# A transformer block on one core: the feed-forward operands are made once without the norm's factor, and its first column block takes the seven-product form too

## The chip, the cores and the metric

The kernel runs on one core of a Trainium2 chip. The core has a matrix engine (PE, which loads weights with its own instructions, PEld), a vector engine (DVE), an activation engine (ACT), a general engine (POOL), and queues that start transfers (SP's, POOL's, ACT's). In the trace each engine runs its instructions in the order in which the program lists them, and waits at an instruction until what it needs is there. The metric is the device time of one execution in microseconds. The kernel before takes 1032.63 us (median of 3 runs, 1032.61 to 1032.65).

## The reference, cut to what matters

256 tokens of width 2048 in fp32 pass one encoder layer:

```
xn = rms_norm(x) * g1;  proj = xn @ w_in        # q, k, v and the convolution's columns
h  = x + concat(attention, convolution) @ w_out
hn = h * rsqrt(mean(h*h) + eps) * g2            # the second norm
y  = h + (silu(hn @ w_gate) * (hn @ w_up)) @ w_down
```

`w_gate` and `w_up` are 2048 x 5632, `w_down` is 5632 x 2048. The factor `rsqrt(...)` is one number for each token. Call it r. It commutes with the product: `hn @ w_gate = r * ((h * g2) @ w_gate)`.

## The kernel before, in words

**Numbers.** Every fp32 operand is split in a high and a low part, and a product is three matmuls: high by high, low by high, high by low. Tokens stand in two halves of 128 (m = 0, 1). A matmul is always 128 x 128 by 128 x 512. The weights come from DRAM as fp32: ACT rounds a raw tile to its high part (`whi`, line 326), DVE subtracts for the low part (`wlo`, line 335); for some tiles the low part is made by ACT and an accumulating transfer of POOL's queue instead (lines 329, 330).

**Chunks.** The program is a list of chunks in the order of PE. A plain chunk is two row tiles of 128 of one weight by 512 columns: 12 matmuls. A loop in `run_chunks` emits, for chunk t, the loads, roundings and splits of the next two or three chunks and then the multiplication of t. Everything that follows from a finished sum (adds, transposes, norms) is a generator, and one step of each running generator is emitted at fixed places within each multiplication (`resume`). So the order on every engine is fixed by this emission, and nothing reorders it later.

**Feed-forward blocks.** There are 11 blocks of 512 hidden columns (j = 0 to 10), in groups of 4, 4 and 3, each group followed by its part of the `w_down` product. Blocks 1 to 10 use a seven-product form on half of the 16 row tiles: four "pairs" (kind s). A pair takes rows p and p + 8 of both `w_gate` and `w_up` and both token halves as a 2 x 2 by 2 x 2 product of tiles, with 7 products in place of 8, so 21 matmuls in place of 24. The other eight row tiles are plain chunks, four of gate (kind g) and four of up (kind u). `ORDER` and `FIRST_ORDER` are strings of these kinds, 12 chunks to a block. For a pair DVE makes sums of weight tiles (`wt`, lines 1049 to 1051), ACT rounds seven tiles (`wh`, lines 1052 and 1055), DVE makes the low parts `wlb` (line 1058) and `wlt` (line 1059). PE's third matmul of a pair reads `wlt`. The sums of the products lie in eight PSUM banks (Q1 to Q7, QX), four of the pool `acc` and four of `aux`. After a block's last pair, `bank_sums` combines banks (one ACT copy, six DVE adds); after its last chunk `block_done` adds two more, multiplies gate and up on DVE, and PE transposes the result (`ps_a`).

**Block 0 before.** It is plain: eight chunks of gate, then eight of up, 192 matmuls. Its token operands `hhi`, `hlo` are the transposed `h * g2`, without r. The silu takes r as its scale (line 876), the product with up takes it again (line 883).

**The operands of blocks 1 to 10 before.** While block 0 runs, `make_forms` builds them from `hn` (the transposed `h * g2`): it spreads r over the partitions by PE (`rep`, `ps_r`, `rb`), multiplies `hn` with it on DVE (line 996), rounds the plain ones (`chi`, `clo`) and builds the seven sums for the pairs (`sums`, `fhi`, `flo`).

**What lies ahead of it.** The product with `w_out` runs in four column blocks n = 0 to 3. For each finished one, `out_done(n)` adds the residual on DVE (line 828), transposes h on PE (`ps_h`, line 846), scales with g2 on ACT (line 851), splits, squares and sums h on ACT (line 479), and writes h to DRAM by POOL's queue (line 823). r exists only after n = 3.

## Time and profile before

| what | number |
|---|---|
| median of 3 runs | 1032.63 us |
| span of the profiled execution | 1030.8 us |
| PE busy, share of the span | 1025.7 us, 100% |
| DVE busy | 929.2 us, 90% |
| ACT busy | 643.4 us, 62% |
| POOL busy | 102.7 us, 10% |
| DMA, mean | 232 GB/s |

The span is 1.8 us short of the runs' median; the same offset is assumed on both sides of the change. Times in the prediction are microseconds from the start of the span. A row of the timeline gives start, duration, engine, line, operation, output<-input, size and count, and in brackets the idle time of the engine ahead of it with what ended it. Two instructions on one engine overlap at their ends, so what a queue takes is read from start to start, not from the durations.

### The profile page before, as it was taken

The numbers are of one execution on the slowest core, as the hardware profiler recorded it, in microseconds if no ns is written. First come the engines' busy times: TensorE is split into PE (matmuls) and PEld (weight loads), VectorE is DVE, ScalarE is ACT, GpSimd is POOL, SyncE is SP. The second block draws the span as 40 slices with busy tenths as digits, with TensorE's granted clock in tenths as the row PEclk, the third lists the DMA queues.
The fourth block names the chain that finished last, engine by engine and source line by source line (L and its number), as shares of the span: only waits on it lengthen the run. The fifth ranks groups of instructions, "written<-read, shape, count | busy, mean of one in ns | idle before, by whom it ended". The sixth has DMA issues, their size and how long they took to land.

```text
span 1030.8 us, 13034 instructions
## 1 busy us (share of the span) xinstructions
PE 1025.7 (100%) x4642; PEld 849.4 (82%) x4642; DVE 929.2 (90%) x1128; ACT 643.4 (62%) x786; POOL 102.7 (10%) x146
## 2 busy tenths in 40 slices
PE   9999999999999999999999999999999999999998
PEld 8888888888888888888888888888888888888887
DVE  6899999999765699999999898989999989889998
ACT  7644656665756675676666556667757556657562
POOL 0300112111000000100102101101001111010020
PEclk9999999999999999999999999999999999999999
DMA  9757555544466677997989799889798979897776
GB/s 338 254 194 258 190 184 164 158 169 166 141 215 214 197 262 222 282 265 210 254 259 272 251 257 270 258 234 262 228 269 255 285 207 283 247 267 218 226 200 174
DMA packets 116448, 238.64 MB, mean 232 GB/s; under 512 B 7840, under 2 KB 9120, under 8 KB 116384
## 3 DMA queue, kind: packets, MB, share of 16 engines
q1 hardware_dynamic: 105216, 203.58, 59.3%
q0 software_dynamic: 10880, 34.08, 17.0%
q8 instruction: 36, 0.59, 0.2%
q14 instruction: 28, 0.23, 0.1%
q10 hardware_dynamic: 288, 0.16, 0.1%
HBM read 204.24 MB, written 9.44 MB: 207 GB/s over the span
## 4 chain that ended last, share of the span: by engine, by line
PE 100%; POOL 0%; DVE 0%; issue 0%; POOLq 0%
PE acc L365 11%; PE acc L366 11%; PE acc L371 11%; PE q L1097 11%; PE q L1103 11%; PE q L1098 11%; PE q L1078 9%; PE q L1077 9%; PE q L1076 9%; PE ps_a L898 1%; PE ps_s L712 1%; PE ps_o L782 1%; PE ps_warm L164 0%; PE ps_h L846 0%; PE ps_qk L693 0%; PE ps_at L802 0%
## 5 line engine op out<-in xcount | busy, mean ns | idle before, releaser
L326 ACT CAST whi<-raw 128x1024 fp32r<-128x1024 f32 (+1 forms) x256 | 264.2, 1043 | 143.8 <-PE acc L366 86.6
L335 DVE TENSOR_TENSOR wlo<-raw,whi 128x1024 fp32r<-128x1024 f32 (+1 forms) x208 | 250.4, 1214 | 38.2 <-ACT whi L326 38.0
L1055 ACT CAST wh<-wt 128x2048 fp32r<-128x2048 f32 x61 | 116.8, 1915 | 109.9 <-DVE wt L1051 109.7
L1059 DVE TENSOR_TENSOR wlt<-wt,wh 128x2048 fp32r<-128x2048 f32 x61 | 139.8, 2291 | 19.8 <-ACT wh L1055 19.7
L1097 PE MATMUL q<-whi,chi 128*128 128x512 f32 x320 | 125.2, 391 | 0.0
L1098 PE MATMUL q<-whi,clo 128*128 128x512 f32 x320 | 124.6, 389 | 0.0
L365 PE MATMUL acc<-whi,xhi 128*128 128x512 f32 x312 | 124.1, 398 | 0.0
L366 PE MATMUL acc<-whi,xlo 128*128 128x512 f32 x312 | 122.2, 392 | 0.0
L1076 PE MATMUL q<-wh,fhi 128*128 128x512 f32 x280 | 109.8, 392 | 0.0
L1077 PE MATMUL q<-wh,flo 128*128 128x512 f32 x280 | 109.0, 389 | 0.0
L1058 DVE TENSOR_TENSOR wlb<-wb,wh 128x1536 fp32r<-128x1536 f32 x61 | 106.8, 1751 | 1.0 <-ACT wh L1052 1.0
L572 DVE SCALAR_TENSOR_TENSOR y<-upad,cw,y 128x256 f32<-128x256 f32 x240 | 101.6, 490 | 0.0
L330 POOL DMA_DIRECT2D wlo<-raw x48 | 41.5, 865 | 555.7 <-ACT wlo L329 286.3
L1052 ACT CAST wh<-wb 128x1536 fp32r<-128x1536 f32 x61 | 89.8, 1472 | 1.0 <-DMA wb<-in_w_down_dram 1.0
L1103 PE MATMUL q<-wlo,chi 128*128 128x512 f32 x320 | 85.7, 390 | 0.0
L371 PE MATMUL acc<-wlo,xhi 128*128 128x512 f32 x312 | 85.2, 394 | 0.0
L1049 DVE TENSOR_TENSOR wt<-wb 128x1024 f32<-128x1024 f32 x61 | 74.4, 1220 | 0.0
L1097 PE MATMUL q<-whi,ahi 128*128 128x512 f32 x182 | 71.0, 390 | 0.0
L1098 PE MATMUL q<-whi,alo 128*128 128x512 f32 x182 | 70.9, 389 | 0.0
L1103 PEld LDWEIGHTS q<-wlo,chi 128*128 128x128 f32 x320 | 60.0, 188 | 12.7 <-DMA wlo<-raw 0.3
L1097 PEld LDWEIGHTS q<-whi,chi 128*128 128x128 f32 x320 | 60.1, 188 | 12.3
L1098 PEld LDWEIGHTS q<-whi,clo 128*128 128x128 f32 x320 | 60.1, 188 | 12.2
(260 smaller groups left out, 1850.5 us busy)
## 6 DMA issues: line engine op xcount, KB each, us to landing
raw<-in_w_in_dram SPq DMA_DIRECT2D x78, 512.0 KB, 4.6
raw<-in_w_gate_dram SPq DMA_DIRECT2D x48, 512.0 KB, 5.0
raw<-in_w_up_dram SPq DMA_DIRECT2D x48, 512.0 KB, 5.3
wlo<-raw POOLq DMA_DIRECT2D x48, 512.0 KB, 7.1
raw<-in_w_down_dram SPq DMA_DIRECT2D x46, 512.0 KB, 6.2
wb<-in_w_down_dram SPq DMA_DIRECT2D x42, 512.0 KB, 5.9
wb<-in_w_up_dram SPq DMA_DIRECT2D x40, 512.0 KB, 4.4
wb<-in_w_gate_dram SPq DMA_DIRECT2D x40, 512.0 KB, 5.5
```

What stands on the lines that cost most here:

```text
L326: act.copy(c["hi"], c["raw"])
L335: dve.tensor_tensor(c["lo"], c["raw"], c["hi"].bitcast(F32), ALU.subtract)
L365: pe.matmul(ps[m], xhi[:, ms], hi[:, j, :], start=c["first"] and j == 0, stop=False)
L366: pe.matmul(ps[m], xlo[:, ms], hi[:, j, :], start=False, stop=False)
L371: pe.matmul(ps[m], xhi[:, ms], lo[:, j, :], start=False, stop=c["last"] and j == nk - 1)
L1055: act.copy(c["hi"][:, :SUMMED], c["t"])
L1059: dve.tensor_tensor(lot, c["t"], c["hi"][:, :SUMMED].bitcast(F32), ALU.subtract)
L1076: pe.matmul(ps, hi, c["hi"][:, w], start=bool(first), stop=False)
L1077: pe.matmul(ps, lo, c["hi"][:, w], start=False, stop=False)
L1097: pe.matmul(ps, xs[i][0][:, ms], hi[:, i, :], start=i == 0 and bool(c["first"].get(qs[m])), stop=False)
L1098: pe.matmul(ps, xs[i][1][:, ms], hi[:, i, :], start=False, stop=False)
L1103: pe.matmul(sum_bank(c, qs[m]), xs[i][0][:, ms], lo[:, i, :], start=False, stop=i == 1 and bool(c["last"].get(qs[m])))
```

## The change

It makes one set of operands for all 11 blocks, from `h * g2` without r. Block 0 becomes a block like the others, with four pairs, in the order `gugsgsgsusuu`. r is applied after the products, in all blocks: the silu takes it as scale, and a second ACT instruction multiplies the silu's result with it, for each token half (`products_done`). The spreading of r, the multiplications with it, and block 0's own operands are gone. Column blocks n = 1 and n = 3 of h are split straight from the transposes (`chi` on ACT, `clo` on DVE); those of n = 0 and 2 are kept as `rows`, and `make_forms` starts after n = 2. None of block 0's low parts goes by a transfer. Which PSUM pool holds which banks is swapped in block 0.

The tiles are also placed anew. The pool of the first phases is closed at n = 0, and the pool of the feed-forward is opened there. What must live longer (h, its scratch, the operands of `w_out`) goes to a pool at the other end of the memory, which is closed after n = 3; `wlb`, `wlt`, the bank sums and the operands of the down product live in a pool (`late`) opened in its place. The first pair can't be rounded in program order before that: `round_pair` runs the generators until `late` exists.

```
-FIRST_ORDER = "gsggsgsuusuu"
+ORDERS = {0: "gugsgsgsusuu", 1: "gsggsgsuusuu"}
...
     def out_done(n, ps):
+        if not n:
+            prestack.close()
+            ffn["pool"] = fp = ctx.enter_context(tc.tile_pool(name="ffn", bufs=1))
+            ffn["rows"] = fp.tile([P, 2, NS, S], F32, tag="wh", name="hn", bufs=2)
...
-            hi, lo = lhs_two("h", k)
-            act.copy(hi, rows)
-            dve.tensor_tensor(lo, rows, hi.bitcast(F32), ALU.subtract)
+            if k % HK < NS:
+                rows = ffn["rows"][:, k // HK, k % HK : k % HK + 2, :]
+                for i in range(2):
+                    act.activation(rows[:, i, :], pt[:, i, :], AF.Copy, scale=col("g2", k + i))
+            else:
...
+                for i in range(2):
+                    act.activation(hi[:, i, :], pt[:, i, :], AF.Copy, scale=col("g2", k + i))
+                for i in range(2):
+                    dve.scalar_tensor_tensor(lo[:, i, :], pt[:, i, :], col("g2", k + i), hi[:, i, :].bitcast(F32),
+                                             ALU.mult, ALU.subtract)
+                    plain[k + i] = (hi[:, i, :], lo[:, i, :])
             yield
         if n < D // N - 1:
             h_squares(n, cs)
-        else:
-            yield
-            yield
-            prestack.close()
-            ffn["pool"] = ctx.enter_context(tc.tile_pool(name="ffn", bufs=1))
+        if n == HK * P // N:
+            yield
             start(make_forms())
+        if n == D // N - 1:
+            yield
+            yield
+            keepstack.close()
+            ffn["late"] = ctx.enter_context(tc.tile_pool(name="late", bufs=1, side="right"))
...
     def round_pair(c):
-        assert "pair" in forms
+        while "pair" not in forms or "late" not in ffn:
+            resume()
...
-            tag, pool_ = ("acc", acc_ps) if i < 4 else ("aux", aux_ps)
+            tag, pool_ = ("acc", acc_ps) if (i < 4) != c["swap"] else ("aux", aux_ps)
...
-        for t in g:
-            act.activation(t, t, AF.Silu)
+        for m, t in enumerate(g):
+            act.activation(t, t, AF.Silu, scale=rstd2[m])
+            act.activation(t, t, AF.Copy, scale=rstd2[m])
...
-            if j:
-                gate_up_block(j)
-                continue
-
-            block(w_gate, j * N, range(KD), fh, silu_done)
-            block(w_up, j * N, range(KD), fh, lambda ps, j=j: up_done(j, ps))
-            chunks[-1]["prompt"] = True
+            gate_up_block(j)
```

Three places show how the instructions moved. The first is PE at the end of the product with `w_out`. The rows are the last matmuls of n = 3 and what follows. Before, a whole chunk of block 0 stands ahead of the first transposes of h:

```order
L371 MATMUL acc<-wlo,mchi_2862 128x512
L371 MATMUL acc<-wlo,mchi_2868 128x512
L371 MATMUL acc<-wlo,mchi_2862 128x512
L365 MATMUL acc<-whi,hhi_2958 128x512
L366 MATMUL acc<-whi,hlo_2959 128x512
...
L371 MATMUL acc<-wlo,hhi_2958 128x512 x4
L846 MATMUL ps_h<-ident,h_81 128x128
L846 MATMUL ps_h<-ident,h_82 128x128
L846 MATMUL ps_h<-ident,h_81 128x128
L846 MATMUL ps_h<-ident,h_82 128x128
L365 MATMUL acc<-whi,hhi_2983 128x512
```

With the change all eight transposes follow the last matmul directly (lines 846 and 852 are the same statement), and block 0 comes after them:

```order
L374 MATMUL acc<-wlo,mchi_2869 128x512
L374 MATMUL acc<-wlo,mchi_2875 128x512
L852 MATMUL ps_h<-ident,h_88 128x128
L852 MATMUL ps_h<-ident,h_89 128x128
...
L852 MATMUL ps_h<-ident,h_88 128x128
L852 MATMUL ps_h<-ident,h_89 128x128
L1066 MATMUL q_3373<-whi,chi 128x512
L1067 MATMUL q_3373<-whi,clo 128x512
```

The chunk that stood between the last matmul of n = 3 and the transposes of its sum is gone from there.

The second place is DVE from the residual add of n = 3 on, with the change. Before, the low part (`wlo`) of block 0's third chunk stood ahead of these adds too, and the rest of block 0's plain low parts and the building of the operands followed them, with the first pair's `wt` behind all of that.

```order
L338 TENSOR_TENSOR wlo<-raw,whi 128x1024 x3
L834 TENSOR_TENSOR h_88<-h_88,acc 128x512
L834 TENSOR_TENSOR h_89<-h_89,acc 128x512
L842 TENSOR_REDUCE ssh<-ss_0_143 128x1
L842 TENSOR_REDUCE ssh<-ss_1_144 128x1
L863 SCALAR_TENSOR_TENSOR clo<-ps_h,cols,chi 128x256 x4
L1018 TENSOR_TENSOR wt<-wb 128x1024
L1019 TENSOR_TENSOR wt<-wb,wt 128x512
L1020 TENSOR_TENSOR wt<-wt,wb 128x512
L338 TENSOR_TENSOR wlo<-raw,whi 128x1024
L1027 TENSOR_TENSOR wlb<-wb,wh 128x1536
L1028 TENSOR_TENSOR wlt<-wt,wh 128x2048
```

The weight work of the first pair now follows the residual add at once, and three more pairs follow it with one `wlo` ahead of each.

The third place is DVE at the change from block 0 to block 1, with the change (the first three rows and `wlb`, `wlt` belong to block 1's first pair, the rows between them to block 0's banks):

```order
L1018 TENSOR_TENSOR wt<-wb 128x1024
L1019 TENSOR_TENSOR wt<-wb,wt 128x512
L1020 TENSOR_TENSOR wt<-wt,wb 128x512
L1157 TENSOR_TENSOR sum_3651<-q_3456,sum_3650 128x512
L1158 TENSOR_TENSOR sum_3652<-q_3460,sum_3651 128x512
L1159 TENSOR_TENSOR sum_3653<-q_3464,sum_3652 128x512
...
L1162 TENSOR_TENSOR sum_3652<-q_3376,sum_3652 128x512
L1027 TENSOR_TENSOR wlb<-wb,wh 128x1536
L1028 TENSOR_TENSOR wlt<-wt,wh 128x2048
L1179 TENSOR_TENSOR sum_3651<-q_3396,sum_3651 128x512
L1179 TENSOR_TENSOR sum_3653<-q_3399,sum_3653 128x512
L1184 TENSOR_TENSOR sum_3651<-sum_3651,sum_3650 128x512
```

Before, block 0 had no banks to sum, and only the two instructions of line 883 stood between the first and the second pair of block 1:

```order
L1049 TENSOR_TENSOR wt<-wb 128x1024
L1050 TENSOR_TENSOR wt<-wb,wt 128x512
L1051 TENSOR_TENSOR wt<-wt,wb 128x512
L335 TENSOR_TENSOR wlo<-raw,whi 128x1024
L1058 TENSOR_TENSOR wlb<-wb,wh 128x1536
L1059 TENSOR_TENSOR wlt<-wt,wh 128x2048
L883 SCALAR_TENSOR_TENSOR a<-acc,rstd_138,sil 128x512 x2
```

Six bank adds moved in ahead of `wlb` and `wlt` of block 1's first pair, and four more instructions behind them.

More of the change, by code (lines that the diff above doesn't have):

```diff
@@ L34 @@
 LINE = 128
+EDGE = 320
 EPS = 1e-6
@@ L804, in attend_values @@
             mixa[2 * hd + e] = lhs_pair("a", 2 * hd + e) if hd >= 2 else tuple(
-                pre.tile([P, S], F32R, tag=t, name=t, bufs=4) for t in ("mahi", "malo"))
+                keep.tile([P, S], F32R, tag=t, name=t, bufs=4) for t in ("mahi", "malo"))
             act.activation(mixa[2 * hd + e][0], pt[:, e, :], AF.Copy, scale=col("sg", e))
@@ L954, in make_down_forms @@
         yield from gap()
-        hs = ffn["pool"].tile([P, 2, nd, P], F32R, tag="dhs", name="dhs")
+        hs = ffn["late"].tile([P, 2, nd, P], F32R, tag="dhs", name="dhs")
         for i, f in ((0, f4), (1, f5)):
@@ L967, in make_down_forms @@
         yield from gap()
-        ls = ffn["pool"].tile([P, 4, nd, P], F32R, tag="draw", name="dls")
+        ls = ffn["late"].tile([P, 4, nd, P], F32R, tag="draw", name="dls")
         act.copy(ls[:, 3], f6)
@@ L1055, in split_pair @@
         act.copy(c["hi"][:, :SUMMED], c["t"])
-        lob = ffn["pool"].tile([P, 7 - SUMMED, N], F32R, tag="wlb", name="wlb", bufs=2)
-        lot = ffn["pool"].tile([P, SUMMED, N], F32R, tag="wlt", name="wlt", bufs=2)
+        lob = ffn["late"].tile([P, 7 - SUMMED, N], F32R, tag="wlb", name="wlb", bufs=2)
+        lot = ffn["late"].tile([P, SUMMED, N], F32R, tag="wlt", name="wlt", bufs=2)
         dve.tensor_tensor(lob, c["b"][:, 1:], c["hi"][:, SUMMED:].bitcast(F32), ALU.subtract)
@@ L1131, in multiply_two, with fast_block @@
             start(c["done"](c["sums"]))
-    def fast_block(order, pairs, twos, sources, operands, half, whole, by_dma=dict(g=(), u=())):
+    def fast_block(order, pairs, twos, sources, operands, half, whole, by_dma=dict(g=(), u=()), swap=False):
         units, sums = [], {}
@@ L1138, in fast_block @@
             what = left[kind].pop(0)
-            c = dict(kind=kind, sums=sums, done=None, first={}, last={}, rows=what["rows"], **operands)
+            c = dict(kind=kind, sums=sums, swap=swap, done=None, first={}, last={}, rows=what["rows"], **operands)
             if kind == "s":
@@ L1183, in bank_sums @@
     def bank_sums(q):
-        w1, u2, u3, w4 = (ffn["pool"].tile([P, N], F32, tag=f"sum{i}", name=f"sum{i}") for i in range(4))
+        w1, u2, u3, w4 = (ffn["late"].tile([P, N], F32, tag=f"sum{i}", name=f"sum{i}") for i in range(4))
         act.copy(w1, q[Q1])
```

87 lines of the change are left out of this document (23 added, 64 removed).

## The prediction

> **What bounds the kernel now.** I read the page's first lines, then PE's waits, then the stages, then the timelines of PE, DVE and ACT from 337 to 432.
>
> ```profile
> PE 1025.7 (100%) x4642; PEld 849.4 (82%) x4642; DVE 929.2 (90%) x1128; ACT 643.4 (62%) x786; POOL 102.7 (10%) x146
> ```
> ```profile
> PE ps_warm L164 <- POOL neghalf L158: 1.4, 1, 1.4
> ```
> The second row is the whole answer on PE's waits: one, at the start. So PE sets the time, and each matmul taken away is a gain as long as its neighbours stay in time. By stages (PE, PEld, DVE, ACT, POOL busy):
>
> ```profile
> 338.00:384.00 46.00, 46.00 (x209) 37.95 (x208) 38.36 (x41) 30.85 (x41) 1.99 (x4) 1.00 0.70 225
> 384.00:427.00 43.00, 43.00 (x195) 35.62 (x194) 41.10 (x38) 28.81 (x26) 3.54 (x4) 1.00 0.85 256
> ```
> The first is block 0, the second block 1, with DVE at 96%. DVE is the next bound, and the change gives block 0 more DVE work than block 1 has. PE's places in the schedule:
>
> ```profile
> 337.40 1.07 PE L371 MATMUL acc<-wlo,mchi 128*128 128x512 f32 x4
> 338.31 0.39 PE L365 MATMUL acc<-whi,hhi 128*128 128x512 f32 x1
> ...
> 341.03 0.67 PE L846 MATMUL ps_h<-ident,h 128*128 128x128 f32 x4
> 341.46 0.48 PE L365 MATMUL acc<-whi,hhi 128*128 128x512 f32 x1
> ...
> 382.20 1.07 PE L371 MATMUL acc<-wlo,hhi 128*128 128x512 f32 x4
> 386.28 0.39 PE L1078 MATMUL q<-wlt,fhi 128*128 128x512 f32 x1
> ```
> From 338.31 to 341.03 PE issues one chunk of 12 matmuls: 2.72, or 0.227 each. The four transposes take 0.43, or 0.108 each. A pair's 21 matmuls take 4.76, and its third, the first that reads `wlt`, comes 0.45 after its start. At 386.28 PE reads block 1's first `wlt`.
>
> ```profile
> 374.82 3.49 DVE L335 TENSOR_TENSOR wlo<-raw,whi 128x1024 fp32r<-128x1024 f32 x3
> 378.23 1.22 DVE L1049 TENSOR_TENSOR wt<-wb 128x1024 f32<-128x1024 f32 x1
> 381.95 1.75 DVE L1058 TENSOR_TENSOR wlb<-wb,wh 128x1536 fp32r<-128x1536 f32 x1
> 383.62 2.29 DVE L1059 TENSOR_TENSOR wlt<-wt,wh 128x2048 fp32r<-128x2048 f32 x1
> 389.41 1.22 DVE L1049 TENSOR_TENSOR wt<-wb 128x1024 f32<-128x1024 f32 x1
> 392.00 1.75 DVE L1058 TENSOR_TENSOR wlb<-wb,wh 128x1536 fp32r<-128x1536 f32 x1
> 394.06 2.29 DVE L1059 TENSOR_TENSOR wlt<-wt,wh 128x2048 fp32r<-128x2048 f32 x1 [0.31 <-ACT wh L1055]
> 396.28 1.22 DVE L335 TENSOR_TENSOR wlo<-raw,whi 128x1024 fp32r<-128x1024 f32 x1
> 397.41 1.22 DVE L1049 TENSOR_TENSOR wt<-wb 128x1024 f32<-128x1024 f32 x1
> 402.06 2.29 DVE L1059 TENSOR_TENSOR wlt<-wt,wh 128x2048 fp32r<-128x2048 f32 x1 [0.31 <-ACT wh L1055]
> ```
> That `wlt` ends at 385.91, so its margin is 0.37: small, but PE never waits. Start to start, DVE needs 1.14 for a `wlo`, 2.59 for the three `wt`, 1.67 for `wlb`, 4.65 from `wt` to `wlt` with the wait for ACT in it (4.3 without), 2.22 for `wlt`; from one pair to the next with one plain chunk between, 8.00 (394.06 to 402.06). PE takes 33 matmuls for the same, 7.48. In a row of such pairs DVE loses 0.52 each time.
>
> **What the change takes away.** Block 0 has 180 matmuls in place of 192: 12 x 0.227 = 2.7. The two transposes that spread r: 2 x 0.108 = 0.2. Together 2.9 off PE. The DVE work on `hn` (line 996, the splits) and ACT's `hhi` also go, but they lay beside PE, which waited for none of it.
>
> **What it adds on PE's path.** First, the transposes of h. Before, a chunk of PE covered the residual add; now they are next on PE, and block 0's matmuls are queued behind them.
>
> ```profile
> 339.83 1.28 DVE L828 TENSOR_TENSOR h<-h,acc 128x512 f32<-128x512 f32 x2
> ```
> ```profile
> 340.54 0.63 ACT L479 ACTIVATE junk<-h 128x512 f32<-128x512 f32 x1 [1.89 <-DVE h L828]
> ...
> 341.93 0.82 ACT L851 ACTIVATE hn<-ps_h,cols 128x256 f32<-128x256 f32 x2
> ```
> The first half's sum is done two matmuls before the end (started 337.40 + 0.23, plus 0.39): 338.02. With the third chunk's `wlo` moved behind it, the add can start at 338.05, the second 0.60 later, done 339.33. One transpose gets through, the other seven then take 0.76: block 0 starts at 340.12. Without waiting, eight transposes would end at 338.31 + 0.86 = 339.17. **Stall 0.95.**
>
> Second, block 0's first pair. Behind the adds DVE waits for ACT: the squares start when the first add ends (338.76), the first `chi` 1.39 later as in the rows above, four of them at 0.42 until 341.85. Then the last two `clo`, priced by the nearest form, a product and subtraction from PSUM of the same size:
>
> ```profile
> L809 DVE SCALAR_TENSOR_TENSOR malo<-ps_at,cols,mahi 128x256 fp32r<-128x256 f32 x4 | 1.7, 480 | 1.6 <-ACT mahi L806 1.6
> ```
> At 0.40 to 0.48 each, `wt` starts at 342.7. Then 2.59, one `wlo` 1.13, `wlb` 1.67, `wlt` 2.29: ready at 350.4. PE, after g, u and g (3 x 2.72), wants it at 340.12 + 8.16 + 0.45 = 348.73. **Stall 1.67.** The three later pairs each have one plain chunk ahead of them, with the DVE period of 8.00 against 7.48: **3 x 0.52 = 1.56.** Block 0 ends on PE at about 384.2, against 383.1 now.
>
> Third, the change to block 1. After the fourth `wlt` starts (372.08) DVE has 2.22, three `wlo` (3.41), the `wt` of block 1's first pair (2.59), and now six bank sums, ahead of `wlb` and `wlt`:
>
> ```profile
> 420.43 0.69 DVE L1188 TENSOR_TENSOR sum<-q,sum 128x512 f32<-128x512 f32 x1
> 423.83 0.68 DVE L1193 TENSOR_TENSOR sum<-q,sum 128x512 f32<-128x512 f32 x1
> ...
> 424.60 1.29 DVE L1209 TENSOR_TENSOR sum<-q,sum 128x512 f32<-128x512 f32 x2
> 425.80 1.28 DVE L1214 TENSOR_TENSOR sum<-sum,sum 128x512 f32<-128x512 f32 x2
> ```
> The six take 4.0 from start to start (420.43 to 423.83 and 0.6). So `wlt` is ready at 372.08 + 2.22 + 3.41 + 2.59 + 4.0 + 1.67 + 2.29 = 388.3; PE wants it at 384.2 + 2.72 + 0.45 = 387.3. **Stall 0.95.** Then four bank instructions (2.4), two `wlo` (2.3), 4.65 and 2.29: the second pair is ready at 399.8. PE, with one pair, two chunks and eight transposes between, wants it at 399.4. **Stall 0.4**, and one more period, **0.5**. After that come two up chunks, one of them split by transfer: 10.2 on PE against 8.0 on DVE, and the debt is gone.
>
> The sum is 0.95 + 1.67 + 1.56 + 0.95 + 0.4 + 0.5 = 6.0 lost, 2.9 won: **+3.1**.
>
> **What I cost at nothing.** The second ACT instruction, 20 times over blocks 1 to 10 and twice in block 0:
>
> ```profile
> 509.27 1.23 ACT L1201 ACTIVATE sum<-sum 128x512 f32<-128x512 f32 x2 [2.07 <-DVE sum L1192]
> 510.95 1.28 DVE L1214 TENSOR_TENSOR sum<-sum,sum 128x512 f32<-128x512 f32 x2
> 514.92 0.60 PE L898 MATMUL ps_a<-ident,sum 128*128 128x128 f32 x4
> ```
> Two more at 0.6 end at about 511.6. The second product of line 1214 starts then anyway (0.6 after 510.95), and PE's transposes come 3.4 after that. The cover is this gap; without it, it would cost at most 11 x 1.2 = 13. Building the operands moves into n = 3:
>
> ```profile
> 330.52 1.23 DVE L335 TENSOR_TENSOR wlo<-raw,whi 128x1024 fp32r<-128x1024 f32 x1 [1.49 <-ACT whi L326]
> 373.15 1.75 DVE L1032 TENSOR_TENSOR flo<-sums,fhi 128x1536 fp32r<-128x1536 f32 x1
> ```
> There DVE idles 1.49 in each chunk, two chunks ahead of need; the largest piece of the building takes 1.75, so a low part comes at most some tenths later than now, and PE notices nothing. If DVE were already full there, the building would delay the residual add by up to its size.
>
> The tiles of the `late` pool wait for h's write to DRAM:
>
> ```profile
> 340.80 1.14 POOL L823 DMA_DIRECT2D hd<-h  x2 [21.66 <-DVE h L828]
> ```
> ```profile
> DMA to landing us min/median/max: 3.9/5.0/6.8
> ```
> The second row is of these writes (line 823). Issued 0.3 after the adds at 0.57 each, so by 340.2, they land at 344 to 347; `wlb` wants it at 346.4, so nothing to 0.6. PE's restart after a wait does not occur in this trace beyond its opening; ACT's handover to an add takes 0.03 (340.54 above), so 0 to 0.1 for each of eight stalls. From below: if ACT's rounding no longer lags, the period is 7.7 and some 1.3 of the loss goes. A gain beyond 2.9 has no source in these rows.
>
> A rule speaks to the stalls themselves. PE's opening shows what a slow clock costs:
>
> ```profile
> 1.35 3.89 PE L164 MATMUL ps_warm<-ident 128*128 128x128 f32 x17 [1.35 <-POOL neghalf L158]
> ```
> 17 transposes take 3.89, against 17 x 0.108 = 1.84 later: 2.0 lost. The Trainium skill (TensorE: Matmul & The Clock Gate, "HAM oscillation — how this bites in real kernels") says that PE falls back to the slow clock after an idle window of about 3.4 us. By that rule none of these stalls, 1.7 at most, does it, and the sum stays +3.1; if the opening's cost came back once, it would be +5.1. No run here shows an idle PE in mid-kernel.
>
> **Rivals.**
> - *DVE keeps up* (the other side). If the pairs' low parts were in time, only the wait for the residual add would stay: -2.9 + 0.95, 1030.7. For it: at block 1's start DVE now arrives within 0.37 and PE has never waited. Against it: DVE's queue cannot begin the first pair before 342.7. It decides from `wlt` ready before 348.73.
> - *Late once, then level.* Only the first two stalls stay, because the sums or ACT's roundings interleave better: -2.9 + 2.6, with some of the 0.52s: 1032.5 to 1033.5, say 1033.2. It needs a period of 7.48, which the rows 394.06 and 402.06 contradict.
> - *More than that*: the slow clock comes back once (+2.0), or h's write lands late at its longest and the loads behind: 1038.5. Against it: the landings above, and for the loads
>
> ```profile
> wb<-in_w_gate_dram SPq DMA_DIRECT2D x40, 512.0 KB, 5.5
> ```
> A pair's tile is free when `wlb` has read it (348.1 for the first) and next wanted by the `wt` two pairs on (359.4): 11 for two loads of 5.5 that overlap.
> - *The full gain.* The add is hidden too: 1029.7. The order of the instructions speaks against it.
>
> That the change doesn't do what it says is excluded by the order: 180 matmuls, and no operand with r.
>
> **How the numbers follow.** The span of 1030.8 becomes 1033.9, the median 1032.63 becomes 1035.7. My chances: forecast 0.68 (its own range, from the bounds above, 1034.2 to 1037.2), keeps up 0.08, late once 0.13, more 0.07, full gain 0.04. The time can be told from no change from 0.2% on, 2.07 us: below 1030.57 or above 1034.70. Faster takes the full gain and a quarter of the first rival: 0.06. Slower takes 0.94 of the forecast and the third rival: 0.71. Same is the rest: 0.23. The range 1032.6 to 1037.8 leaves out the first and the last rival and most of the third.
>
> **What would show it.** Right: PE's waits list `ps_h` on the residual add (about 1), `q<-wlt` on DVE's `wlt` seven times (1.7, three of 0.5, 0.95, 0.4, 0.5), and no more from block 2 on; matmuls of 128 x 512 fall by 12. Wrong: PE without waits (first rival), waits on whi, on wb's loads or on POOL (third), matmuls at 0.43 after a stall (the clock), or waits in each block at `ps_a` (the second ACT instruction).

## The result, and the profile after

The changed kernel takes 1038.13 us (median of 4 runs, 1037.33 to 1038.45) against 1032.62 for the kernel before, a ratio of 1.0053 (95% interval 1.0039 to 1.0067). A second set of runs gave 1037.80 against 1032.50, 1.0050 (1.0036 to 1.0063). Three executions among all the runs of this document, of 1476.94, 1733.16 and 2683.64 us, lie far above the others of their kernels and are left out of every median and count. So the change is 5.5 us slower, where 3.1 slower was forecast: the sign was right, the time lies above the range (1032.6 to 1037.8). The profiled execution took 1038.45, with a span of 1036.7; by spans the loss is 5.9.

The page's first line and the answer on PE's waits, after the change (us in total, times, longest):

```profile
PE 1027.2 (99%) x4628; PEld 847.2 (82%) x4628; DVE 941.2 (91%) x1142; ACT 658.3 (64%) x796; POOL 102.4 (10%) x146
...
PE ps_h L852 <- DVE h L834: 1.7, 2, 1.5
PE ps_warm L167 <- POOL neghalf L161: 1.4, 1, 1.4
PE q L1047 <- DVE wlt L1028: 1.3, 4, 0.6
PE q L1072 <- DMA wlo<-raw: 0.7, 1, 0.7
```

14 matmuls fewer (12 of 128x512 and two transposes), and in place of one wait there are now waits on the residual add, on `wlt` and on a transfer. Line numbers of the changed kernel: `wlo` 338, residual add 834, `ps_h` 852, `chi` 861, `clo` 863, `wt` 1018 to 1020, `wlb` 1027, `wlt` 1028, a pair's matmuls 1045 to 1047, plain ones 1066 to 1072, silu and the second ACT instruction 1170 and 1171. Where an experiment adds lines, its numbers are a few higher; rows are told by their names.

**The first wait** is longer than forecast since the add is late. DVE and ACT while the operands are built, then the add:

```profile
327.01 1.23 DVE L338 TENSOR_TENSOR wlo<-raw,whi 128x1024 fp32r<-128x1024 f32 x1
328.15 0.68 DVE L989 TENSOR_TENSOR sums<-hn 128x512 f32<-128x512 f32 x1
331.85 1.23 DVE L338 TENSOR_TENSOR wlo<-raw,whi 128x1024 fp32r<-128x1024 f32 x1 [1.21 <-ACT whi L329]
335.87 3.48 DVE L338 TENSOR_TENSOR wlo<-raw,whi 128x1024 fp32r<-128x1024 f32 x3
339.28 1.28 DVE L834 TENSOR_TENSOR h<-h,acc 128x512 f32<-128x512 f32 x2
```
```profile
328.87 1.48 ACT L992 CAST fhi<-sums 128x1536 fp32r<-128x1536 f32 x1 [1.89 <-DVE sums L989]
330.77 2.95 ACT L329 CAST whi<-raw 128x1024 fp32r<-128x1024 f32 x3
```

ACT waits 1.89 for `sums`, which stand behind a `wlo` in DVE's queue; the next `whi` stands behind that rounding in ACT's queue; and DVE then waits 1.21 for this `whi`. From 331.85 on DVE is busy without a gap and reaches the add at 339.28. Forecast was 338.05.

**PE then runs slowly for a while**, and reaches the first pair just as its `wlt` comes. PE's rows, the `wlt` on DVE, and the granted clock by windows (the number before the last two):

```profile
340.01 0.33 PE L852 MATMUL ps_h<-ident,h 128*128 128x128 f32 x1 [1.48 <-DVE h L834]
340.61 1.39 PE L852 MATMUL ps_h<-ident,h 128*128 128x128 f32 x7 [0.27 <-DVE h L834]
343.50 0.63 PE L1066 MATMUL q<-whi,chi 128*128 128x512 f32 x1
343.93 0.63 PE L1067 MATMUL q<-whi,clo 128*128 128x512 f32 x1
351.45 0.39 PE L1046 MATMUL q<-wh,flo 128*128 128x512 f32 x1
351.69 0.47 PE L1047 MATMUL q<-wlt,fhi 128*128 128x512 f32 x1
```
```profile
349.19 2.29 DVE L1028 TENSOR_TENSOR wlt<-wt,wh 128x2048 fp32r<-128x2048 f32 x1
357.19 2.29 DVE L1028 TENSOR_TENSOR wlt<-wt,wh 128x2048 fp32r<-128x2048 f32 x1 [0.31 <-ACT wh L1024]
365.19 2.29 DVE L1028 TENSOR_TENSOR wlt<-wt,wh 128x2048 fp32r<-128x2048 f32 x1 [0.32 <-ACT wh L1024]
```
```profile
340.00:343.40 3.40, 3.12 (x12) 2.64 (x13) 2.04 (x6) 3.37 (x9) 1.99 (x4) 0.65 0.90 262
343.40:346.80 3.40, 3.40 (x14) 2.71 (x14) 3.33 (x6) 1.18 (x2) 0.00 (x0) 0.84 0.74 285
```

Matmuls of 128x512 come at 0.43 in place of 0.227 from 341.65, the first of them, until 344.4. The first `wlt` is ready at 349.19 + 2.29 = 351.48, PE's second matmul of the pair starts at 351.45, so no wait is listed there. From pair to pair DVE takes 8.00, as forecast.

**Later** three more terms: block 1's first pair waits, a low part made by transfer lands late, and between block 2 and the end some 0.8 goes.

```profile
389.38 0.50 PE L1047 MATMUL q<-wlt,fhi 128*128 128x512 f32 x1 [0.63 <-DVE wlt L1028]
418.73 1.20 PE L1072 MATMUL q<-wlo,chi 128*128 128x512 f32 x4 [0.67 <-DMA wlo<-raw]
```

The table gives PE's times counted from the start of `w_out`'s last four low-part matmuls (337.40 before, 337.47 after), since the opening of the kernel varies by some tenths from one execution to the next. Columns: the first matmul that reads `wlt`, of block 0's four pairs and of block 1's first; the first transposes of `ps_a` in block 2; the start of PE's last row. All from PE's timeline of one profiled execution each; the forecast row is the prediction's own steps (350.40, 358.40, ..., 388.3) less 337.40.

| kernel | pair 1 | pair 2 | pair 3 | pair 4 | block 1 | block 2 | end |
|---|---|---|---|---|---|---|---|
| before | - | - | - | - | 48.88 | 92.22 | 689.25 |
| forecast | 13.00 | 21.00 | 29.00 | 37.00 | 50.9 | 95.3 | 692.4 |
| the change | 14.22 | 22.07 | 30.07 | 38.07 | 51.91 | 97.26 | 695.07 |
| wait filled | 14.20 | 22.04 | 30.04 | 38.04 | 51.89 | 96.25 | 694.17 |
| no `wlb` in block 0 | 13.42 | 21.36 | 29.35 | 37.35 | 51.19 | 95.62 | 693.40 |
| both | 13.42 | 21.36 | 29.35 | 37.34 | 51.19 | 95.56 | 693.32 |
| building half a chunk later | 13.08 | 20.92 | 28.92 | 36.92 | 50.76 | 95.33 | 693.51 |
| `wt` ahead of `wlo` | 14.20 | 21.80 | 29.49 | 37.20 | 51.05 | 94.75 | 692.80 |
| operands alone | - | - | - | - | 48.65 | 91.98 | 689.74 |
| one more plain chunk first | 16.69 | 25.88 | 33.36 | 40.84 | 54.69 | 98.64 | 696.39 |
| all orders, extra chunk | 14.55 | 22.15 | 29.84 | 37.56 | 50.24 | 94.62 | 692.29 |
| all orders, change's sequence | 11.67 | 19.27 | 26.96 | 34.67 | 48.52 | 92.25 | 689.91 |
| the same, four low parts by transfer | 11.66 | 19.23 | 27.45 | 34.93 | 47.85 | 91.20 | 694.06 |
| all orders, r in the product | 11.67 | 19.27 | 26.96 | 34.68 | 48.53 | 92.38 | 690.36 |
| the same, two low parts by transfer | 11.67 | 19.27 | 26.96 | 36.54 | 49.49 | 92.81 | 694.76 |

The change is 1.22 behind the forecast at the first pair, 1.0 behind at block 1, 2.0 behind at block 2 and 2.7 at the end. What lies between is what the experiments are about.

### The profile page after: what moved, and what is told of

The parts are those of the page before. It is cut to its first block, busy times and chain, and to the rows that moved or that the text cites. A ratio compares the mean times of both kernels' runs of the same rounds, so it can differ in the third digit from the quotient of the medians.

```text
span 1036.7 us, 13005 instructions
## 1 busy us (share of the span) xinstructions
PE 1027.2 (99%) x4628; PEld 847.2 (82%) x4628; DVE 941.2 (91%) x1142; ACT 658.3 (64%) x796; POOL 102.4 (10%) x146
## 4 chain that ended last, share of the span: by engine, by line
PE 82%; DVE 8%; issue 4%; DMA 3%; ACT 2%; SPq 0%; DVEq 0%; POOLq 0%; ACTq 0%
PE acc L368 9%; PE acc L369 9%; PE acc L374 9%; PE q L1072 9%; PE q L1066 9%; PE q L1067 9%; PE q L1047 8%; PE q L1046 8%; PE q L1045 8%; DVE wlo L338 2%; DMA wlo<-raw 2%; ACT wh L1024 1%; DVE wt L1018 1%; DVE wlt L1028 1%; DVE wt L1019 1%
## 5 line engine op out<-in xcount | busy, mean ns | idle before, releaser
L329 ACT CAST whi<-raw 128x1024 fp32r<-128x1024 f32 (+1 forms) x248 | 255.9, 1043 | 130.6 <-PE acc L369 76.3
L338 DVE TENSOR_TENSOR wlo<-raw,whi 128x1024 fp32r<-128x1024 f32 (+1 forms) x200 | 239.6, 1209 | 35.3 <-ACT whi L329 35.1
L1024 ACT CAST wh<-wt 128x2048 fp32r<-128x2048 f32 x65 | 124.5, 1915 | 126.0 <-DVE wt L1020 125.9
L1028 DVE TENSOR_TENSOR wlt<-wt,wh 128x2048 fp32r<-128x2048 f32 x65 | 148.9, 2291 | 20.7 <-ACT wh L1024 20.6
L1066 PE MATMUL q<-whi,chi 128*128 128x512 f32 x352 | 138.6, 394 | 0.0
L1067 PE MATMUL q<-whi,clo 128*128 128x512 f32 x352 | 137.7, 391 | 0.0
L1045 PE MATMUL q<-wh,fhi 128*128 128x512 f32 x308 | 120.7, 392 | 0.0
L1046 PE MATMUL q<-wh,flo 128*128 128x512 f32 x308 | 119.9, 389 | 0.0
L1027 DVE TENSOR_TENSOR wlb<-wb,wh 128x1536 fp32r<-128x1536 f32 x65 | 113.8, 1751 | 1.0 <-ACT wh L1021 1.0
L1072 PE MATMUL q<-wlo,chi 128*128 128x512 f32 x352 | 94.3, 390 | 0.8 <-DMA wlo<-raw 0.7
```

Of the source, the lines that this page charges most:

```text
L329: act.copy(c["hi"], c["raw"])
L338: dve.tensor_tensor(c["lo"], c["raw"], c["hi"].bitcast(F32), ALU.subtract)
L1024: act.copy(c["hi"][:, :SUMMED], c["t"])
L1028: dve.tensor_tensor(lot, c["t"], c["hi"][:, :SUMMED].bitcast(F32), ALU.subtract)
L1045: pe.matmul(ps, hi, c["hi"][:, w], start=bool(first), stop=False)
L1046: pe.matmul(ps, lo, c["hi"][:, w], start=False, stop=False)
```

## The experiments

The medians of the first four runs differ from the change's by 0.1%, which is as much as the intervals are wide; their verdicts rest on the times in the traces, and the medians only agree.

The theory at the outset (A): block 0 has two delays side by side at its first pair, the slow clock on PE and the late chain on DVE, so that only the longer counts; behind it, DVE sets the pace. The first rival (B): the slow clock is a cost of its own. The second (C): the loss has nothing to do with DVE's load in block 0.

### Filling PE's wait

```
             pt = aux_ps.tile([P, 2, S], F32, tag="aux", name="ps_h")
+            if n == 3 and not t:
+                for _ in range(12):
+                    pe.transpose(pt[:, 0, :P], ident, ident)
```

> The change, with 12 more 128x128 transposes of the identity (0.108 us each, 1.3 us) on PE between the last product of w_out and the transposes of h, so that PE does not sit idle for the residual add and its clock is not lowered. Theory A (two delays side by side: in block 0 PE's matmuls at half rate cost about 1.9 us, but the first pair's wlt from DVE, ready at 351.48, holds PE back to the same moment): granted clock 1.00 in 340 to 347, the 1.9 us come back as a wait for wlt before the first pair, time as in the change, 1037.8 to 1038.4. Theory B (the slow clock is a cost of its own): 1036.2, no new wait for wlt.

1037.21 us, ratio 1.0046 (1.0031 to 1.0061). The windows and PE's rows at the first pair:

```profile
340.00:343.40 3.40, 3.13 (x18) 2.69 (x18) 2.04 (x7) 3.37 (x9) 1.96 (x4) 1.00 0.91 270
```
```profile
349.57 0.39 PE L1049 MATMUL q<-wh,flo 128*128 128x512 f32 x1
351.41 0.47 PE L1050 MATMUL q<-wlt,fhi 128*128 128x512 f32 x1 [1.45 <-issue]
```

The clock stays up, PE is 1.6 early at the first pair and waits there for `wlt`: 14.20 in the table against 14.22. So the slow clock cost nothing up to there, as theory A says, and theory B falls for this place. The median is nevertheless 0.9 lower, more than A expected. In the table the two part only between block 1's pairs and block 2 (51.89 and 51.91, then 96.25 and 97.26): there the transfer of the row at 418.73 was late in the change and not in this run. Over the nine executions of the change in both sets, six have a mean granted clock of 0.997 or 0.998 and take 1038.1 on average, three have 1.000 and take 1037.3. That the slow clock makes that transfer late is not shown; one profiled execution of each is too few.

### Taking `wlb` out of block 0, and both

```
+        lob = c["hi"][:, SUMMED:]
...
-        dve.tensor_tensor(lob, c["b"][:, 1:], c["hi"][:, SUMMED:].bitcast(F32), ALU.subtract)
+        c["swap"] or dve.tensor_tensor(lob, c["b"][:, 1:], c["hi"][:, SUMMED:].bitcast(F32), ALU.subtract)
```

> The change without DVE's low parts wlb in the four pairs of block 0 (line 1027, 1.75 us each; the products take the high part in their place, so that part of the computation is changed). Theory A: PE reaches the first pair at 351.45 in any case because of the slow clock, so 0.25 is won there; the waits of 0.2 to 0.4 at the other three pairs go (1.0 us), the wait of 0.8 at block 1's first pair too and perhaps the two of 0.4 behind it: 1.5 to 2.6 faster than the change, 1035.5 to 1036.6. Theory B: the same. A rival C (the loss is in the operands or the pools and not in DVE's load in block 0): no change, 1038.1.

> Both of these edits at once. Theory A: the two delays cover one another at the first pair, so that together they win more than the sum of the two: some 1.4 to 1.9 beyond the second one alone, 1034.0 to 1035.0. Theory B: the sum of the two, with 1.9 of it from the filled wait and that already seen alone: 1034 too, but then the first of these runs is at 1036.2. Rival C: 1036 to 1038.

1037.00 (ratio 1.0044, 1.0029 to 1.0059) and 1036.76 (1.0042, 1.0026 to 1.0058): both miss their expectation, and this miss was the useful one. At the first pair 0.8 is won, but behind it the pairs still come every 7.94 to 8.0, though DVE has 1.67 less to do for each:

```profile
353.68 0.69 DVE L1020 TENSOR_TENSOR wt<-wt,wb 128x512 f32<-128x512 f32 x1
356.35 2.29 DVE L1030 TENSOR_TENSOR wlt<-wt,wh 128x2048 fp32r<-128x2048 f32 x1 [1.97 <-ACT wh L1024]
```

DVE now idles 1.97 where `wlb` stood: it waits for ACT to round `wt`. So the period isn't DVE's amount of work. It is a loop through two engines: `wlo` (1.13), `wt` (2.6), ACT's rounding (1.92), `wlt` (2.2), one behind the other, 8.0 with the handovers. `wlb` lay in the shadow of ACT's rounding all along. In the change it covers all of that shadow but 0.31. And in this execution the wait of 1.45 before `ps_h` left the clock at 1.00 in 340.0 to 343.4, so the same wait lowers it in one execution and not in another. The run with both edits therefore had nothing more to win by the filled wait, and its row in the table is the same to 0.1.

### Building the operands half a chunk later

```
         yield
+        yield
         act.copy(fhi[:, 4:7], f[:, 4:7])
```

> The change with half a chunk more between building the sums of the operands (DVE) and rounding them (ACT): ACT rounds the next weight chunk first and does not wait 1.9 us for DVE's sums ahead of it, so DVE does not sit idle 1.2 us behind ACT. Theory A (the residual add came 1.2 late because ACT and DVE waited for one another while the operands were built): the add starts at about 338.1 in place of 339.28, PE waits 0.3 to 0.5 before the transposes and not 1.5, its clock stays at 1.00, wlt of the first pair is ready 1.1 earlier: 1.0 to 1.3 faster than the change, 1036.8 to 1037.1. If DVE's queue was full by the amount of work and not by that wait, the add stays at 339.3 and the time at 1038.1.

1036.84, ratio 1.0041 (1.0026 to 1.0056), as expected. The add comes when it was forecast, and PE waits 0.33 and 0.27 in place of 1.48 and 0.27:

```profile
338.18 1.28 DVE L834 TENSOR_TENSOR h<-h,acc 128x512 f32<-128x512 f32 x2
```
```profile
338.92 0.33 PE L852 MATMUL ps_h<-ident,h 128*128 128x128 f32 x1 [0.33 <-DVE h L834]
```

Pair 1 comes at 13.08; the forecast had 13.00. Nothing was taken away, one rounding was let past another. The late add was the two engines' waiting for one another, not the amount of work on DVE, and it cost 1.1 at the first pair.

### `wt` ahead of `wlo`

In the loop that emits the chunks, where the next chunk to be rounded is a pair, its `wt` now goes ahead of the split of the plain chunk before it:

```
             hi_lead, lo_lead = lead(t)
+            if i < min(n, t + 1 + hi_lead) and chunks[i].get("kind") == "s":
+                load(i)
+                ...
+                chunks[i]["round"](chunks[i])
+                i += 1
             while j < min(i, t + 1 + lo_lead):
```

> The change with one step of the order turned round in every block: where a pair is to be rounded next, DVE makes its sums wt (2.6 us) before the low part wlo of the plain chunk ahead of it (1.13), so that wlo and wlb (2.8) run while ACT rounds wt (1.92). Theory D (the pairs of block 0 come every 8.0 us not since DVE has too much to do, but since wlo, wt, ACT's rounding and wlt stand one behind the other: 1.13 + 2.6 + 1.92 + 2.21, with the handovers 8.0; without wlb the pairs still came at 8.0): the period falls to 7.6, the waits at the second to fourth pair from 0.25 to 0.4 to about 0.1 each, those at block 1's second and third pair too: 0.9 to 1.3 faster than the change, 1036.0 to 1037.0, the first pair's wait unchanged. Theory A as it stood (DVE's amount of work sets the period): the same work in another order, 8.0, no gain: 1037.3 to 1038.4.

1035.98, ratio 1.0032 (1.0019 to 1.0046): about 2 us less than the change, more than expected. DVE in block 0:

```profile
354.31 1.22 DVE L338 TENSOR_TENSOR wlo<-raw,whi 128x1024 fp32r<-128x1024 f32 x1
355.44 1.75 DVE L1034 TENSOR_TENSOR wlb<-wb,wh 128x1536 fp32r<-128x1536 f32 x1
357.12 2.29 DVE L1035 TENSOR_TENSOR wlt<-wt,wh 128x2048 fp32r<-128x2048 f32 x1
364.84 2.28 DVE L1035 TENSOR_TENSOR wlt<-wt,wh 128x2048 fp32r<-128x2048 f32 x1
```

The wait for ACT is gone from DVE's rows and the pairs come every 7.72 (357.12 to 364.84): the same work, in another order. This is now DVE's own work without a gap, and PE's 7.48 is 0.24 away. At pair 4 the change is 0.87 behind this run, at block 2 it is 2.5 behind. 1.0 of that is the late transfer, the rest (0.6) the same loop in block 1.

### The operands alone

Made in the kernel before: `make_forms` without `rep`, `ps_r`, `rb` and the multiplications, and r behind the products; block 0 plain, pools as they were.

```
...
-        for t in g:
-            act.activation(t, t, AF.Silu)
+        for m, t in enumerate(g):
+            act.activation(t, t, AF.Silu, scale=rstd2[m])
+            act.activation(t, t, AF.Copy, scale=rstd2[m])
```

> One part of the change alone, made in the kernel before: the operands of the pairs are built from h without the second norm's factor (no rep, ps_r and rb, no multiplication by rb), and silu and a second ACT instruction take the factor in the product, while block 0 stays plain and the pools stay where they were. If the loss is in the pairs of block 0 alone: within 0.5 of before, 1032.1 to 1033.0 (PE does two transposes less, 0.2). If the second ACT instruction or the operands cost something in each block: 1034 or more.

1033.18, ratio 1.0006 (0.9997 to 1.0015): a little above the first of the two ranges, and not to be told from before by its time. Its trace says more: up to block 2 it is 0.24 ahead of before (the two transposes), from there to the end it takes 597.76 against 597.03. Every kernel with the second ACT instruction takes 597.7 to 598.2 there, but for the one told of below whose last pass waits for loads.

### One plain chunk more ahead of the first pair

```
-ORDERS = {0: "gugsgsgsusuu", 1: "gsggsgsuusuu"}
+ORDERS = {0: "gugusgsgsusu", 1: "gsggsgsuusuu"}
```

> The change with block 0's units in the order g u g u s g s g s u s u in place of g u g s g s g s u s u u: one plain chunk more ahead of the first pair, and the residual add has that chunk (2.72 us) as cover. Theory A: the wait before the transposes falls from 1.5 to 0.5 or less, the first pair's wlt comes 1.1 later (one more wlo) while PE has 2.72 more to do, so 1.5 to 2 are won there; the later pairs still come at 8.0 and wait 0.3 to 0.4 each: 1036.0 to 1036.8. If both delays only move on to the next pair: 1038.

1039.49, ratio 1.0067 (1.0053 to 1.0081): slower than the change, and no theory had that. The wait before `ps_h` fell to 0.3, but the first pair came 2.47 later and not 1.1 as expected, so that of the 2.72 more that PE has to do ahead of it only 0.25 covered anything. The add came 1.1 later, DVE waited 0.80 more for ACT's `chi` ahead of the last low parts, and `wlb` waited 0.35 for the transfer that writes h to DRAM. PE waited 2.9 for the first pair (3.15 from start to start, less one matmul of 0.23). Also, block 0 now ended with one u chunk in place of two behind its last pair. Block 1's first products need the PSUM banks that block 0's sums must first be read from:

```profile
385.95 0.50 PE L1066 MATMUL q<-whi,chi 128*128 128x512 f32 x1 [0.73 <-ACT sum L1155]
387.45 0.50 PE L1066 MATMUL q<-whi,chi 128*128 128x512 f32 x1 [0.77 <-DVE sum L1157]
```

The chunk that covers the add at the front had covered the sums at the back. Behind both places PE was slow in this execution, 0.43 for each matmul of 128x512 from 354.5 to 357.4 and again from 388.5 to 391.9:

```profile
353.88 0.47 PE L1047 MATMUL q<-wlt,fhi 128*128 128x512 f32 x1 [2.76 <-issue]
355.31 0.63 PE L1045 MATMUL q<-wh,fhi 128*128 128x512 f32 x1
388.90 0.63 PE L1067 MATMUL q<-whi,clo 128*128 128x512 f32 x1
```

The second stretch cost 1.6: the nine matmuls from 388.49 to 391.88 start 3.39 apart in place of 1.82, and the `wlt` that the last of them reads had been ready at 386.80, so nothing on DVE lay beside it. There the slow clock was a cost of its own, as theory B had it for another place. How much of the median it makes is not shown: three of the four executions have a mean clock of 0.996, and the one with 1.000 took 1039.86.

### All the orders at once, with and without that chunk

Both have the two orders above (operands built half a chunk later, `wt` ahead of `wlo`) and two more steps: the residual add is emitted right behind `w_out`'s last product, and the first pair's `wt` no longer waits in program order for the `late` pool, so that the transposes come in the middle of the first plain chunk. The first of the two has the extra chunk as well.

```
     block(w_out, 3 * N, range(16), fm, lambda ps: out_done(3, ps))
+    chunks[-1]["prompt"] = True
...
-        while "pair" not in forms or "late" not in ffn:
+        while "pair" not in forms:
             resume()
...
         act.copy(c["hi"][:, :SUMMED], c["t"])
+        while "late" not in ffn:
+            resume()
```

> The change with all the orders at once: the half chunk between sums and rounding of the operands, wt before wlo, one more plain chunk ahead of the first pair, and the first pair's wt and DVE's residual add put ahead of the work that PE needs later (the add right behind w_out's last product, the transposes in the middle of the first plain chunk). Nothing is left out of the computation. Theory A with D: no wait at the transposes, none or up to 0.5 at the first pair, 0.1 at the others, up to 0.8 at block 1's first pair; the 2.9 us of matmuls that block 0 saves come through but for that: 1030.0 to 1031.5, faster than before by 1 to 2.5. If there is another limit that these waits hid (loads, ACT, the sums at block 0's end): 1033 to 1035.

> The run with all the orders, but block 0's units in the change's own order again (g u g s g s g s u s u u), since the extra plain chunk ahead of the first pair left one u chunk too few at the end, and block 1's first products waited 1.7 for the sums of block 0. Theory E (what is left is DVE's own work: 7.73 a pair against PE's 7.48, and the first pair's wlt at the end of a queue without gaps): wlt of the first pair at 349.3, 1.2 after PE wants it, 0.25 and a slow first product at each of the three others, 0.8 at block 1's first pair: 1032.6 to 1034.0. If the wait for the sums stays at 1.7 with this order too, it has another cause: 1035 or more.

With the extra chunk 1035.90 (1.0033, 1.0020 to 1.0045): PE waited 1.7 for the sums at block 1's start and 1.4 for the first pair (from start to start, less one matmul), so the other limit of the expectation was there, and the time lies above the range given for it too. Without it 1033.11, ratio 1.0006 (0.9998 to 1.0015), as expected. PE does not wait before `ps_h` at all, and at the first pair

```profile
347.59 0.39 PE L1056 MATMUL q<-wh,flo 128*128 128x512 f32 x1
349.06 0.47 PE L1057 MATMUL q<-wlt,fhi 128*128 128x512 f32 x1 [1.08 <-issue]
```

it waits 1.24 (1.47 less one matmul of 0.23). At block 2 it is at 92.25, where the kernel before is at 92.22. So the order of the instructions alone, with all the change's work done, brings back 4.7 of the 5.3 us by which the change was slower in this comparison. The 2.9 that PE saves in block 0 are spent on what is left: the 1.24, 0.1 or less at each of the three pairs behind it, 0.8 at block 1's first pair, and the slower first matmul after each wait.

### Low parts by transfer in block 0

```
-                   BY_DMA if j > 1 and j not in FIRSTS else dict(g=(), u=BY_DMA["u"] if j else ()), swap=not j)
+                   BY_DMA if j > 1 and j not in FIRSTS else dict(g=() if j else TWOS[2:], u=BY_DMA["u"]), swap=not j)
```

> The same, with block 0's low parts of the third and fourth g chunk and of the second and fourth u chunk made by ACT and an accumulating transfer, as in later blocks, and not by DVE (1.13 each). Theory E: DVE's period falls to 6.8 and PE never waits at the second to fourth pair (0.75 won, with the restarts 1.0), block 1's first pair waits less: 1031.0 to 1032.5, so as fast as before or up to 0.15% faster. If the transfers land late (8.8 us in block 1 of the change): waits for DMA in block 0, 1033 to 1035.

1037.52 (five runs, 1034.76 to 1038.11), ratio 1.0040 (1.0027 to 1.0052). The wait at block 1's first pair is gone, and block 2 is reached at 91.20, 1.0 ahead of before: the part of the reasoning about DVE is right. But the time misses the expectation. Within block 0 one of the four transfers landed 0.6 late (pair 3 at 27.45), and most is lost at the other end of the kernel, in the last pass with `w_down`; there a pair's weights come late, DVE waits 3.8 for them and PE 2.4 for DVE:

```profile
1009.98 1.23 DVE L1026 TENSOR_TENSOR wt<-wb 128x1024 f32<-128x1024 f32 x1 [3.83 <-DMA wb<-in_w_down_dram]
```

Behind that wait PE runs at 0.43 for each matmul from 1018.4 to 1021.4. Three of the five executions have a mean clock of 0.998 and take 1037.5 to 1038.1, two have 0.999 and take 1034.8 and 1034.9.

### The change once more

> The change as it is, once more, beside these two. If the slow clock after the wait for the residual add is what happens in most executions of this kernel: granted clock 0.998 in most of them, and those with 1.000 some 0.3 to 1.1 faster, 1037.3 to 1038.5. If it was chance: 1.000 in most, and 1037.3.

1037.80, ratio 1.0050 (1.0036 to 1.0063); clocks of 0.997 or 0.998 in three executions, 1.000 in two. So the slow clock comes in more than half of them, not in all.

### r in DVE's product, then two low parts by transfer

```
-            act.activation(t, t, AF.Copy, scale=rstd2[m])
...
-            dve.tensor_tensor(u[m], u[m], g[m], ALU.mult)
+            dve.scalar_tensor_tensor(u[m], u[m], rstd2[m], g[m], ALU.mult, ALU.mult)
```

> The kernel of the run with the orders and without the extra chunk (1033.1), with the factor taken in DVE's product, u times r times silu in one instruction of the form that the residual's low parts have (0.69 for 128x512 against 0.68), in place of the second ACT instruction in each block. The prediction put that ACT instruction at nothing. In the traces the part from block 2 to the end takes 597.0 in the kernel before and 597.7 to 598.1 in every kernel with the second ACT instruction, the operands alone included; 0.4 of it is a wait for wlt at the start of each of the first two down passes, where ACT scales (0.72 + 0.72) ahead of the rounding of wt. If the second instruction is the cause: those two waits go, 1032.3 to 1032.7. If not: 1033.1, and the waits stay.

> The same, with the low parts of the second and fourth u chunk of block 0 made by ACT and an accumulating transfer, as in later blocks. Block 1's first pair then has 1.1 less of DVE's work ahead of its wlt: its wait of 0.8 goes, block 2 starts 91.4 behind w_out's last low parts (92.25 without): 1031.4 to 1032.0, faster than before by 0.1%. If the loads of the last down pass come late again, as in the run with four such transfers (8 us into its last pass DVE waited 3.8 for them): 1034 to 1037, with that wait there and block 2 early all the same.

The first gives 1032.50, ratio 1.0004 (0.9995 to 1.0013), as expected. That is 0.6 less than without; each taken against the kernel before of its own set (0.61 and 0.18 above it), it is 0.4, and the intervals overlap, so the cause rests on the traces. The end of block 3 on ACT and DVE, first with the second ACT instruction (the run with all orders and the change's sequence), then with r in the product:

```profile
509.28 0.72 ACT L1180 ACTIVATE sum<-sum,rstd 128x512 f32<-128x512 f32 x1 [2.06 <-DVE sum L1171]
510.04 0.72 ACT L1181 ACTIVATE sum<-sum,rstd 128x512 f32<-128x512 f32 x1
510.67 0.71 ACT L1180 ACTIVATE sum<-sum,rstd 128x512 f32<-128x512 f32 x1
511.41 0.73 ACT L1181 ACTIVATE sum<-sum,rstd 128x512 f32<-128x512 f32 x1
```
```profile
510.96 0.68 DVE L1194 TENSOR_TENSOR sum<-sum,sum 128x512 f32<-128x512 f32 x1
512.17 0.69 DVE L1194 TENSOR_TENSOR sum<-sum,sum 128x512 f32<-128x512 f32 x1 [0.53 <-ACT sum L1181]
512.78 1.22 DVE L1026 TENSOR_TENSOR wt<-wb 128x1024 f32<-128x1024 f32 x1
```
```profile
510.77 1.41 DVE L1193 SCALAR_TENSOR_TENSOR sum<-sum,rstd,sum 128x512 f32<-128x512 f32 x2
512.10 1.22 DVE L1026 TENSOR_TENSOR wt<-wb 128x1024 f32<-128x1024 f32 x1
```

DVE's second product waits 0.53 for ACT, and behind it in the queue stands the `wt` of the first pair of the down pass. PE's first `wlt` there came at 519.78 after a matmul at 519.26, 0.29 late; with r in the product it is on time, and so is the one at the second down pass. The table's end of 690.36 for this run has a late transfer in it (0.97 at 508) that the run without r in the product did not have. The next kernel, with r in the product too, has no such transfer. From block 2 to a matmul shortly ahead of its late loads (1013.27) it takes 583.01, where the kernel before takes 583.09 and the run with the second ACT instruction 583.77. The kernel of this first run is the best version found: as fast as the kernel before within what can be measured, and none of these beats it.

The second gives 1036.56 (1035.84 to 1038.28), ratio 1.0043 (1.0029 to 1.0057), in the range of the expectation's other case. Two transfers in block 0 go with what four went with: the last down pass waits again. The loads of `wb` there are issued at the same moments as without (996.56 and 996.84), but the slower of the two lands after 13.5 in place of 9.2. Landing times of these two loads, without and with:

```profile
DMA to landing us min/median/max: 7.0/8.1/9.2
```
```profile
DMA to landing us min/median/max: 6.9/10.2/13.5
```

In the run with four transfers the slower one took 13.5 too, in the twelve other kernels 9.2 to 9.9, by one profiled execution of each. Why transfers in block 0 should move the landing of loads issued at 997 is open; the instructions of the last pass are the same. In block 0 itself one of the two landed 1.7 late too (pair 4 at 36.54), so block 2 came at 92.81 and not at 91.4, though the wait of 0.8 at block 1's first pair was gone.

## Why the prediction was wrong, point by point

- **What is won, 2.9**: right. 14 matmuls fewer, and the kernel with the operands alone is 0.24 ahead at block 2 by its two transposes.
- **The wait before `ps_h`, 0.95: the step that failed first.** It took the add at 338.05; it came at 339.28. The prediction had put the building of the operands at nothing, "a low part comes at most some tenths later", and gave the other case as DVE being full. Neither held: DVE and ACT waited for one another (1.89 and 1.21) and that made DVE late. Letting one rounding past the other brought the add to 338.18. The price, 1.1 to 1.2, went through to the first pair and from there to the end.
- **The first pair, 1.67**: the chain from the add to `wlt` was right (351.48 - 339.28 = 12.2; forecast 350.4 - 338.05 = 12.35). As a wait it didn't appear, since the slow clock took its place; with the clock at 1.00 it was 1.61 (the row at 351.41).
- **The slow clock**: costed at nothing with the Trainium skill's rule (TensorE: Matmul & The Clock Gate, "HAM oscillation — how this bites in real kernels": an idle window of about 3.4 us). The trace disagrees with that as a bound: after a wait of 1.48 and one of 0.27 the granted clock was 0.65 in the next 3.4 us, in six of nine executions of the change the mean was below 0.999, and after 1.45 in another kernel it stayed at 1.00. So a wait of half that length can lower it, and need not. That the sum came out right without it up to the first pair was luck: the slow stretch lay beside DVE's lateness (14.22 and 14.20). In the run with one more plain chunk a slow stretch at block 1's start lay beside nothing and cost 1.6.
- **Three pairs at 8.00 against 7.48, 1.56**: the size was right (8.00 from 349.19 to 357.19 to 365.19; PE lost 0.37, 0.52 and 0.52 from pair to pair). The reason was half right. The prediction called it DVE's need, and noted that it would be 7.7 if ACT's rounding no longer lagged: that is what the turned order showed, 7.72, and without `wlb` 8.0 remained.
- **Block 1's first pair, 0.95**: 51.91 - 38.07 = 13.84 from pair 4; forecast 13.9. Then 0.4 and 0.5: in the trace 11.54 and 8.00 to the next two pairs, against 11.12 and 7.50 before, so 0.42 and 0.50.
- **"The debt is gone" behind that: failed.** One of block 1's low parts by transfer landed 0.67 late and cost PE 0.83, with the slow restart 1.0 (11.30 to the next pair, 10.33 with the wait filled). It is not in every execution: with the wait filled PE lost nothing there. What makes the transfer late stays open.
- **The second ACT instruction at nothing: failed, by some 0.8.** The prediction let two more instructions end at 511.6, each at 0.6. From start to start Silu to Copy on one tile takes 0.76 and 0.74, Copy to the next tile's Silu 0.63 (509.28, 510.04, 510.67, 511.41), so they end at 512.1, and DVE's second product, behind which the next pair's `wt` stands, waits 0.53. It costs PE only where the next chunk is a pair of the down pass: 0.29 and a slower first matmul, twice. In the profiled execution of the change the first of the two is hidden beside a transfer that lands late (PE loses 0.42 at 512.86), and only the second, at 773.95, is seen.
- **h's write to DRAM and the pools**: no wait of that kind in the trace of the change; right. With one more plain chunk `wlb` waited 0.35 for it, within the "nothing to 0.6" of the prediction.

The sum by spans: forecast 3.1; the late add 1.2; the transfer in block 1 1.0 (0.67 idle, with what follows it); the second ACT instruction 0.8 (half of it seen as the late transfer at 512.86 that hides it); the other steps take back 0.2: 5.9. So the late add is shown by the run that moves one rounding and the second ACT instruction by the two runs without it, while the transfer is seen in the trace and its cause is not known. Of the rivals the third, with the slow clock or late transfers and 1038.5, came nearest in time. Its slow clock was not what cost the time up to the first pair, and the transfer that came late was neither h's write nor a load of `wb`, which it had named.

## What to carry to other kernels

Where two engines in order feed one another, add up the loop through both (work on one, handover, work on the other), not each engine's busy time: taking work from the busier one left the time from pair to pair as it was (8.0 and 8.0), and emitting an independent instruction into the gap brought it to 7.72 and won some 1.5 us up to block 2. Before costing an added instruction at nothing because its engine has room, look at what stands behind its consumer in the consumer's queue. And where two delays lie side by side, filling one shows only the other: the trace tells this from a cause that isn't there, by a new wait in place of the old delay (1.45 at the first pair here).

## What the runs showed of the hardware that was not expected

- After a wait of 1.5 us PE ran at about half its rate for the next 2.7 us (0.43 for each 128x512 from 341.65 to 344.4), and in three of nine executions of the change the mean clock shows no such stretch. In single profiled executions the same came after waits of 2.9 us, 2.4 us, and two of 0.7 to 0.8 us close together, and did not come after waits of 1.6, 1.45 and 1.24 us. With 12 transposes put into the wait the mean granted clock was 0.999 or 1.000 in all executions.
- The first matmul after a wait is followed by the next one after 0.34 in place of 0.227 (359.54 to 359.88, 389.38 to 389.72), after the longer waits 0.31 (349.06 to 349.37 in the run with all orders): about 0.1 for each restart. The prediction allowed 0 to 0.1.
- A Copy behind a Silu on the same tile starts 0.74 to 0.76 after it, a Silu on another tile 0.63 after that Copy (128x512, the ACT rows from 509.28 on). Whether the shared tile makes the difference is not tested.
- With two or four accumulating transfers more in block 0, a load some 620 us later landed after 13.5 us in place of 9.2, in the profiled execution of each of the two kernels that had them. The cause stays open.
